# A transformer block on one core: last output chunk by hand, weight norms asked for later, gated values stored as float16 parts, down projection in float16

## The chip, the core and the metric

One core of a Trainium2 chip runs one program. Its engines are TensorE (PE, matrix products), VectorE (DVE), ScalarE (ACT) and GpSimd (POOL); SyncE (SP) issues the transfers that are spoken of here. The metric is the device time of one execution in microseconds (us), as the median of the runs shown.

## The reference, cut to what matters

One layer of a block with two mixing paths and a gated MLP, over 2048 latent tokens of width 1024, with 256 context tokens beside them. The inputs are float32.

```python
h  = modulate(x, norm1_g, sh1, sc1)                 # RMSNorm, scale, shift
...                                                 # attention and delta rule -> o_attn, o_gdn
lat_out = jnp.concatenate([o_attn, o_gdn], axis=-1) @ w_out      # 1024 x 1024
x = x + g1 * lat_out
x = x + g2 * conv_ffn(modulate(x, norm2_g, sh2, sc2), w_up, ffn_conv_w, ffn_conv_b, w_down)
return rms_norm(x, final_norm_g)

def conv_ffn(h, w_up, conv_w, conv_b, w_down):      # w_up 1024 x 5632, w_down 2816 x 1024
    u = depthwise_conv(h @ w_up, conv_w) + conv_b   # width 3 over tokens, centred
    gate, val = jnp.split(u, 2, axis=-1)
    return (jax.nn.silu(gate) * val) @ w_down
```

The change lies in the last three stages: output projection, up projection with conv and gate, down projection with the final norm.

## The kernel before

Everything is kept transposed: 128 features on the partitions, tokens along the free axis. The tokens are cut into four chunks of 512; `cb`, `b` and `k` count blocks of 128 features. A float32 factor is held as two parts, `hi` and `lo` (the rounding error of `hi`), and a product is three matmuls: hi·hi, hi·lo, lo·hi (`prods`; L522, L523, L524 in the down projection).

**Output projection** (`output`, recorded by `Plan`, issued by a planner through L404, which is the line of everything that it issues). For each chunk, in the order 1, 2, 0, 3, and each block `cb`: 24 float32r matmuls into `po`, the gated residual into `xv` (DVE), squares for the second norm. The weights come as `raw_o` and are split into `ws_o` by ACT and POOL. `norm_tail` normalises a finished chunk and writes it to `h2c` in DRAM. During chunk 3, `early` builds seven operand blocks `blk0` for the first 1024 tokens: `B11 T2 T1 B21 T3 T4 B22`, made of sums and differences of `h2c` chunks 0 and 1 and each split into two float16 parts. `late_blocks` builds `blk1` for the other 1024 tokens in the second up step.

**Up projection** (`up_stage`, order written by hand). Step (j, sb) computes gate block j and value block j of 128 hidden features for 1024 tokens; there are 44 steps. Instead of eight 512-column block products it does seven (a Winograd form of Strassen's scheme): P1, P6, P4, P3, P5, P2, P7, of 12 float16 matmuls of 512 columns each (`product`, L1829), where P4 and P3 belong to the step before. Their sums go from the banks `ua`, `ub`, `uc` into the rows `ue` (in the trace part of `xa`). `after` then applies the conv as three taps (ACT L1896, DVE L1899), the gate (ACT L1905, DVE L1906), and stores the float32 product in `hidc` (L1907). `prep` gets the weights of the next j ready beside it, one `next(work)` per product: squares of the two loads `raw_u` on ACT (L1585), their sum over partitions by one PE matmul into `uns` (L1588), a scale by it, and seven sums of quarters, each split by ACT and POOL into `ws_u` (`put`, `split`, L1574 and L1577). `fetch_up` loads the next `raw_u` once `prep` of a j is through. Three buffers are there for `raw`, four for `ws`.

**Down projection**. `units` are (chunk, block b, part): per chunk 8 blocks, each of 22 k in parts of 8, 8 and 6. `fetch` loads a unit's weights `raw_d` two units ahead, `leading` (ACT) and `rest` (DVE) split them into float32r parts `ws_d`. `load_part` loads the gated values of a chunk, one k at a time, as `hraw`, and splits each into `hid` (ACT L1815, DVE or POOL L1816). At the end of a chunk `last_norm` squares, sums (`nps_f`, PE), spreads the reciprocal root over the partitions (`nrs_f`, PE) and scales (`finish`); the program drains it at the end of the next unit group. The final chunk is 514 columns wide (the conv reaches over) and is worked in two cuts.

A generator's `next` writes its next piece into the program. Each engine works through its own instructions in the order in which they were written; SP's transfers are one queue.

## Time and profile before

The kernel takes 3633.89 us (median of 3 runs, 3632.43 to 3639.54). The profiled execution took 3634.78 us, its span is 3633.0.

| what | profiled execution |
|---|---|
| granted clock, mean | 0.947 |
| PE busy | 3252.4 us, 90% |
| weight loads (PEld) | 2300.8 us, 63% |
| DVE busy | 2264.1 us, 62% |
| ACT busy | 1727.6 us, 48% |
| POOL busy | 1656.3 us, 46% |
| moved | 374.96 MB, 103 GB/s |
| input projection, attention, delta rule | 0 to about 1755 us |
| output projection, chunks 1, 2, 0 | to 1970.5 us |
| chunk 3 and up steps one to three | 1970.5 to 2150.4 us |
| rest of the up projection | 2150.4 to 3018.8 us |
| down projection (first matmuls inside the stage before) | 2999.8 to 3633.0 us |

How to read it: a busy share is the time in which an engine had an instruction running, so a PE that runs at a low granted clock is busy as well; the clock is given as a share of the full one. In a listing, `out<-in` are the names of the buffers, `<-ACT junk L1585` after a time in brackets is the idle time just before the instruction and what ended it, and L-numbers are lines of the kernel.

### The profile page before, as it was taken

Reading aid. Unit: us, or ns where it says so; the run is one execution under the profiler, and the core shown is the slowest. Engines: PE = TensorE matmul, PEld = TensorE weight load, DVE = VectorE, ACT = ScalarE, POOL = GpSimd, SP = SyncE. Lnnn points to the kernel's source line nnn. Section 1 sums busy time; section 2 is a strip of 40 time slices with the busy share of each in tenths; the row PEclk is TensorE's granted clock in tenths of the full one; section 3 lists DMA queues with packets and bytes.
Section 4 is the critical chain, followed back from the end, with each engine's and each line's share of the span. In section 5 each row is a group of like instructions: output and inputs, shape, how many; then the busy total and the mean of one; then the engine's idle time right before and its main releaser. Section 6 shows DMA issues by size and latency. Waiting matters only on the chain.

```text
span 3633.0 us, 63480 instructions
## 1 busy us (share of the span) xinstructions
PE 3252.4 (90%) x25544; PEld 2300.8 (63%) x25544; DVE 2264.1 (62%) x3403; ACT 1727.6 (48%) x2676; POOL 1656.3 (46%) x1494
## 2 busy tenths in 40 slices
PE   6899999889999999999788579999989996987988
PEld 3799788757777777776566334444434444766878
DVE  5664678787777788887455655665655654334343
ACT  5442333467777777776434543444334433222231
POOL 5684555557777777777554432233322221000000
PEclk8899999999999999999899789999999998988999
DMA  6222435622222233221355421111111124444452
GB/s 225 86 73 87 134 121 159 185 92 71 75 96 67 98 103 92 85 79 56 125 195 208 147 70 47 47 53 47 53 58 47 47 73 129 125 151 147 128 163 88
DMA packets 217366, 374.96 MB, mean 103 GB/s; under 512 B 21368, under 2 KB 96728, under 8 KB 216800
## 3 DMA queue, kind: packets, MB, share of 16 engines
q1 hardware_dynamic: 215120, 365.50, 31.2%
q0 software_dynamic: 1952, 5.42, 0.6%
q8 instruction: 200, 3.28, 0.4%
q14 instruction: 94, 0.77, 0.1%
HBM read 260.06 MB, written 111.20 MB: 102 GB/s over the span
## 4 chain that ended last, share of the span: by engine, by line
PE 57%; DVE 17%; DMA 11%; POOL 6%; ACT 5%; issue 3%; SPq 1%; POOLq 0%; ACTq 0%; DVEq 0%
PE uc L1829 6%; PE sc L404 6%; PE ub L1829 5%; PE ops L404 5%; DVE cv L1899 4%; PE pdn L522 4%; PE pdn L524 4%; PE pdn L523 4%; PE po L404 4%; DMA hraw<-hidc 3%; DMA raw_u<-in_wu 3%; PE ua L1829 3%; PE sm L404 2%; PE pa L404 1%; DVE mx L404 1%
## 5 line engine op out<-in xcount | busy, mean ns | idle before, releaser
L404 POOL TENSOR_TENSOR lp<-p,hp 128x1024 f16<-128x1024 f32 x288 | 622.0, 2168 | 215.5 <-DVE hp L404 68.7
L1829 PEld LDWEIGHTS <-ws_u 128*128 128x128 f16 x3696 | 374.3, 102 | 504.2 <-issue 82.4
L404 DVE TENSOR_REDUCE mx<-sm 128x1 f32<-128x512 f32 x512 | 336.6, 682 | 65.8 <-PE sm L404 64.0
L404 ACT ACTIVATE p<-sc 128x1024 f32<-128x1024 f32 x288 | 295.3, 1025 | 138.8 <-PE sc L404 124.7
L522 PE MATMUL pdn<-hid,ws_d 128*128 128x512 f32 (+2 forms) x880 | 319.0, 363 | 20.8 <-ACT hid L1815 20.7
L523 PE MATMUL pdn<-hid,ws_d 128*128 128x512 f32 (+2 forms) x880 | 315.0, 358 | 5.6 <-DVE hid L1816 3.3
L524 PE MATMUL pdn<-hid,ws_d 128*128 128x512 f32 (+2 forms) x880 | 313.6, 356 | 0.0
L1899 DVE SCALAR_TENSOR_TENSOR cv<-xa,ufw,cv 128x1024 f32<-128x1024 f32 (+1 forms) x176 | 258.9, 1472 | 66.5 <-ACT cv L1896 63.3
L1829 PE MATMUL ua<-blk,ws_u 128*128 128x512 f16 x1056 | 246.1, 383 | 13.2 <-ACT blk L1574 7.5
L1816 POOL TENSOR_TENSOR hid<-hraw,hid 128x512 fp32r<-128x512 f32 (+1 forms) x24 | 29.3, 1220 | 476.7 <-ACT hid L1815 456.0
L404 PE MATMUL sc<-q,kh 128*128 128x512 f16 x576 | 219.0, 380 | 4.7 <-ACT p L404 3.5
L404 PE MATMUL sc<-qx,kx 128*128 128x512 f16 x576 | 219.2, 381 | 0.0
L404 PE MATMUL po<-ol,ws_o 128*128 128x512 f32 x768 | 201.1, 422 | 15.1 <-ACT ws_o L404 9.0
L1577 POOL TENSOR_TENSOR ws_u<-raw_u,ws_u 128x512 f16<-128x512 f32 x105 | 143.4, 1374 | 149.0 <-ACT ws_u L1574 149.0
L1896 ACT ACTIVATE cv<-xa,cols,ufw 128x1024 f32<-128x1024 f32 (+1 forms) x88 | 108.6, 1238 | 206.6 <-DVE xa L1887 201.8
L522 PEld LDWEIGHTS pdn<-hid,ws_d 128*128 128x128 f32 x880 | 170.6, 194 | 50.9 <-ACT hid L1815 25.8
L404 ACT CAST hp<-p 128x1024 f16<-128x1024 f32 x192 | 201.1, 1048 | 3.6
L404 PE MATMUL ops<-vst,hp 128*128 128x65 f16 (+1 forms) x4608 | 192.5, 194 | 7.0 <-DVE hp L404 3.3
L523 PEld LDWEIGHTS pdn<-hid,ws_d 128*128 128x128 f32 x880 | 170.5, 194 | 36.2 <-DVE hid L1816 7.4
L404 PEld LDWEIGHTS po<-ol,ws_o 128*128 128x128 f32 x768 | 154.3, 204 | 55.9 <-ACT ws_o L404 9.4
L404 PEld LDWEIGHTS <-hp 128*128 128x128 f16 x4608 | 170.6, 98 | 24.1 <-DVE hp L404 5.0
L524 PEld LDWEIGHTS pdn<-hid,ws_d 128*128 128x128 f32 x880 | 170.3, 194 | 23.4
(666 smaller groups left out, 8153.2 us busy)
## 6 DMA issues: line engine op xcount, KB each, us to landing
raw_d<-in_wd SPq DMA_DIRECT2D x64, 512.0 KB
raw_u<-in_wu SPq DMA_DIRECT2D x44, 512.0 KB
tk<-gsc SPq DMA_DIRECT2D x34, 512.0 KB
tT<-gsc SPq DMA_DIRECT2D x66, 256.0 KB
hraw<-hidc SPq DMA_DIRECT2D x66, 256.0 KB
wm<-in_wm SPq DMA_DIRECT2D x64, 256.0 KB
gsc<-kd SPq DMA_DIRECT2D x64, 256.0 KB
raw_o<-in_wo SPq DMA_DIRECT2D x32, 512.0 KB
```

Of the source, the lines that this page charges most:

```text
L404: fn(**{k: v.get() if isinstance(v, Lazy) else v for k, v in kw.items()})
L522: PE.matmul(out=ps, lhsT=hi_l(k), rhs=hi_r(k), start=st, stop=False)
L523: PE.matmul(out=ps, lhsT=hi_l(k), rhs=lo_r(k), start=False, stop=False)
L524: PE.matmul(out=ps, lhsT=lo_l(k), rhs=hi_r(k), start=False, stop=en)
L1577: lo_e.tensor_tensor(out=dst[1], in0=src, in1=dst[0], op=ALU.subtract)
L1816: (G if k % 3 == 2 else V).tensor_tensor(out=at[:, 1, k, :W], in0=raw, in1=at[:, 0, k, :W].bitcast(F32), op=ALU.subtract)
L1829: PE.matmul(out=ps, lhsT=w[:, x, k, :], rhs=b[:, y, k, :], start=first and k + f == 0, stop=k == 3 and f == 2, skip_group_check=True)
L1896: S.activation(out=c, in_=t[:, 0:W], func=AF.Identity, scale=s.fw[:, 3 * r:3 * r + 1], bias=cols[:, C_FB + b:C_FB + b + 1])
L1899: V.scalar_tensor_tensor(out=c, in0=t[:, i:i + W], scalar=s.fw[:, 3 * r + i:3 * r + i + 1], in1=c, op0=ALU.mult, op1=ALU.add)
```

## The change

It has these parts.

- *Output projection.* The planned part does chunks 1, 0, 2. Chunk 3 is written by hand (`last_output`): after every second k of its matmuls come one step of three generators, which build `blk0` in two groups of k (`blocks`), do the norm of chunk 2 and the weights of j = 0, and the scales of j = 1.
- *Up projection.* `prep` becomes `scales` and `parts_of`; two `next` per product are taken, not one. `scales` squares, then idles four calls before `uns`, adds 16 matmuls that give each weight column's norm, idles three calls, and scales. The loads `raw_u` are written earlier, and 22 loads `raw_n` of 512 KB (`wd_squares`) give the norms of the down weights' rows.
- *Gated values.* From the column norms comes a bound `bet` of each gated row; the conv's taps of the value rows are scaled by it, and `after` stores the product as two float16 parts. The second 1024 tokens' rows are one column wider; that column, 511 of chunk 1, is kept in `tailc`.
- *Down projection.* The weights are multiplied by `wds` (DVE, L1935) and split into float16 parts, fetched three units ahead; `raw` has four buffers. `load_hid` fetches a chunk's values, a chunk ahead, in four transfers without a split; for chunk 1 it copies `tailc` into column 511. Only the last block is cut in two. `last_norm` has empty calls between its pieces. The output is stored one column to the right, with single-column stores at the chunk borders.

The diff, cut to this:

```diff
-    RAWB, WSB, OLW = 3, 4, 514
+    RAWB, WSB, XW = 4, 4, 514
...
+    def scales(j, tag):
...
+            junk.append(s3.tile([P, 2, 4, P], BF16, tag=tag, name=f"junk_{j}_{r}", bufs=2))
+            S.activation(out=junk[r], in_=t, func=AF.Square, accum_out=ss[:, r:r + 1])
+            yield
+        yield from idle(4)
+        ps = pt3.tile([P, 512], F32, tag="pt", name=f"uns_{j}")
+        PE.matmul(out=ps[:, 0:2], lhsT=ones, rhs=ss, start=True, stop=True, skip_group_check=True)
+        for r in range(2):
+            for k in range(8):
+                PE.matmul(out=ps[:, 2 + 2 * r:4 + 2 * r], lhsT=junk[r][:, k // 4, k % 4, :], rhs=ones16, ...)
...
+        yield from idle(3)
+        for t in (g, v):
+            S.activation(out=t, in_=t, func=AF.Copy, scale=sg[:, 3:4])
+            yield
...
+    def last_output(xv2, acc2, ol, xv, ready):
...
+        first = chained(blocks(0, blk, 0, True), blocks(0, blk, 1, True))
+        second = chained(idle(4), norm_tail(direct, xv2, 2, acc2, s3, h2c[2], 3), scales(0, "osq"), idle(1), parts_of(0))
+        third = chained(idle(19), scales(1, "osq"))
...
+                if k % 2:
+                    next(first, None)
+                    next(second, None)
+                    next(third, None)
...
     def leading(u):
-            made[u] = w3.tile([P, 2, 8, P], F32R, tag="ws", name=f"ws_d{tb}_{b}_{a}", bufs=WSB)
+            made[u] = w3.tile([P, 2, 8, P], F16, tag="ws", name=f"ws_d{tb}_{b}_{a}", bufs=WSB)
+            V.tensor_tensor(out=raws[u][:, :n], in0=raws[u][:, :n], in1=wds[:, a:a + n].unsqueeze(2).broadcast_to([P, n, P]),
+                            op=ALU.mult)
             S.copy(out=made[u][:, 0, :n], in_=raws[u][:, :n])
...
-            fetch(u + 2)
+            fetch(u + 3)
...
+    def load_hid(c, i):
...
+        if c == 1:
+            for t, a, n in got:
+                V.tensor_copy(out=t[:, 0:n, :, 511], in_=tailc[:, a:a + n, :])
...
     def after(s):
...
-            SY.dma_start(out=hidc[s.j, :, 1024 * s.sb:1024 * s.sb + W], in_=cv[1])
+            z = c.bitcast(F16).rearrange("p (f t) -> p f t", f=2)
+            S.copy(out=z[:, 0, :W], in_=v)
+            V.tensor_tensor(out=z[:, 1, :W], in0=v, in1=z[:, 0, :W], op=ALU.subtract)
+            if sb:
+                G.tensor_copy(out=tailc[:, j, :], in_=z[:, :, 0])
+            for i in range(2):
+                SY.dma_start(out=hidc[2 * sb + i, :, j], in_=z[:, :, sb + 512 * i:sb + 512 * i + 512])
...
+            elif n >= 4 and sb == 0 and j < NJ - 3:
+                drain(work)
+                if n == 4:
+                    fetch_up(3)
+                work = chained(idle(4 if n == 4 else 0), made_up(j + 1), wd_squares(j))
...
     def last_norm(x2, tb, acc):
-        ps = norm_sums(psn, "nps", acc, 512, f"f{tb}")
-        yield
-        rs = rep_rstd(Direct(nc), psn, "nps", 1, s4, 2, ps, 512, f"f{tb}")
-        yield
-        finish(x2, tb, (0, 512), rs)
-        yield
+        yield
+        ps = sums(psn, "nps", acc, 512, f"f{tb}")
+        dg = rstd_made(direct, s4[0], ps, 512, f"f{tb}")
+        yield
+        yield
+        rs = rstd_spread(direct, psn, "nps", 1, dg, 512, f"f{tb}")
+        yield
+        finish(x2, tb, (0, 512), rs, range(0, 4))
+        yield
+        finish(x2, tb, (0, 512), rs, range(4, KT))
+        yield
...
+        load_hid(1, 0)
+        load_hid(1, 1)
         for u, (tb, b, a, n) in enumerate(units):
...
+                if b == 0:
+                    if 0 < tb < NCH - 1:
+                        load_hid(tb + 1, 0)
+                        load_hid(tb + 1, 1)
```

In the order of the instructions this shows at three places. A row is line, operation, `out<-in` with the number of each buffer, and shape; x2 stands for two in a row.

PE in step (3, 0), before: the norm of the weights j = 4 (`uns_4`, of `uss_4`) between the last product into `ub` of step (2, 1) and its last into `uc`.

```order
L1829 LDWEIGHTS ws_u2_1_30230
L1829 MATMUL ub_2_1_30536<-xb_29933,ws_u2_1_30230 128x512
L1588 MATMUL uns_4_30698<-uss_4_30663,k32_76 128x2
L1829 LDWEIGHTS ws_u2_1_30230
L1829 MATMUL uc_2_1_30589<-xa_29796,ws_u2_1_30230 128x512
```

PE there, after:

```order
L1998 LDWEIGHTS ws_u2_1_30363
L1998 MATMUL uc_2_1_30675<-xa_29815,ws_u2_1_30363 128x512
L1753 MATMUL uns_4_30807<-uss_4_30755,k32_76 128x2
L1756 LDWEIGHTS junk_4_0_30758
L1756 MATMUL uns_4_30807<-ones16_27906,junk_4_0_30758 128x2
```

The norm now stands one product later, behind `uc`, and 16 small matmuls with the squares `junk` follow it.

SP about the same steps, before: the stores of gated values (`hidc`) and the weights' loads (`raw_u`).

```order
L1907 DMA hidc_71<-cv_3_1_1_31001 128x1026
L1907 DMA hidc_71<-cv_4_0_1_31132 128x1024
L1630 DMA raw_u6_0_31157<-in_wu 128x1024
L1630 DMA raw_u6_1_31158<-in_wu 128x1024
L1907 DMA hidc_71<-cv_4_1_1_31266 128x1026
```

SP there, after:

```order
L2085 DMA hidc_71<-cv_3_0_0_30975 128x2x512 x2
L2085 DMA hidc_71<-cv_3_1_0_31102 128x2x512 x2
L1738 DMA raw_u6_0_31257<-in_wu 128x1024
L1738 DMA raw_u6_1_31259<-in_wu 128x1024
L2097 DMA raw_n4_31279<-in_wd 128x8x128
L2085 DMA hidc_71<-cv_4_0_0_31274 128x2x512 x2
```

The loads of j = 6 moved ahead of the store of step (4, 0), the load `raw_n4` stands behind them, and each store is two.

DVE at the border of the up and the down projection, before: the last taps (`cv_21`), sums of the last step, and splits of gated values loaded for chunk 0 (`hid_0`).

```order
L1899 SCALAR_TENSOR_TENSOR cv_21_0_1_35645<-xa_29796,ufw_21_35170,cv_21_0_1_35645 128x1024 x2
L1906 TENSOR_TENSOR cv_21_0_1_35645<-cv_21_0_0_35619,cv_21_0_1_35645 128x1024
L1878 TENSOR_TENSOR u3_21_1_35682<-ub_21_1_35557,s1_21_1_35542 128x512
L1879 TENSOR_TENSOR xa_29796<-uc_21_1_35632,u3_21_1_35682 128x512
L1883 TENSOR_TENSOR xa_29796<-ub_21_1_35557,s1_21_1_35542 128x512
L1887 TENSOR_TENSOR xa_29796<-uc_21_1_35632,u2_21_1_35570 128x512
L1816 TENSOR_TENSOR hid_0_1_35711<-hraw_0_8_35712,hid_0_1_35711 128x512
```

DVE there, after:

```order
L2055 TENSOR_TENSOR xa_29815<-uc_21_1_36330,u2_21_1_36298 128x512
L2069 SCALAR_TENSOR_TENSOR cv_21_1_0_36417<-xa_29815,ufw_21_35735,cv_21_1_0_36417 128x1025 x2
L2069 SCALAR_TENSOR_TENSOR cv_21_1_1_36421<-xa_29815,ufw_21_35735,cv_21_1_1_36421 128x1025
L1967 COPY hid_1_36443<-tailc_27907 128x32
L2069 SCALAR_TENSOR_TENSOR cv_21_1_1_36421<-xa_29815,ufw_21_35735,cv_21_1_1_36421 128x1025
L1967 COPY hid_1_B22_36447<-tailc_27907 128x8
L2077 TENSOR_TENSOR cv_21_1_1_36421<-cv_21_1_0_36417,cv_21_1_1_36421 128x1025
L2081 TENSOR_TENSOR cv_21_1_0_36417<-cv_21_1_1_36421,cv_21_1_0_36417 128x1025
L1967 COPY hid_1_hx_36448<-tailc_27907 128x4
L1935 TENSOR_TENSOR raw_d0_0_16_36139<-raw_d0_0_16_36139,wds_27932 128x768
L1942 TENSOR_TENSOR ws_d0_0_16_36458<-raw_d0_0_16_36139,ws_d0_0_16_36458 128x768
```

The splits of gated values are gone; between the last taps stand three copies of `tailc` into the buffers of chunk 1, and behind them the weights of the third unit. PE has at this place the products of the last step, with the first two units of the down projection (43 matmuls into `pdn_0_0`) between P7 and the last two, P4 and P3.

More of the change, by code (lines that the diff above doesn't have):

```diff
@@ L1779, in output @@
-        plan.issue(dict(o=("work", 1.0)))
-        up_w[0] = {m: t.get() for m, t in at.items()}, fw.get()
-        return xv.get(), acc.get(), {m: t.get() for m, t in blk0.items()}
+            if n < 2:
+                pend = norm_tail(plan, xv, tb, acc, s3, h2_l[tb])
+        for _ in range(2):
+            ready.append(weights(*wts.pop(0)))
+        x_end = mk(x3, [P, KT, 512], F32, "x", "x3_3", 2)
+        for k in range(0, KT, 2):
+            SY.dma_start(out=x_end[:, k:k + 2, :], in_=xt[3][:, k:k + 2, :])
@@ new lines, in output, with chained, idle, fetch_up @@
+        plan.keep([xv, acc, nxt, x_end] + ready)
+        plan.issue(dict(o=("work", 1.0)))
+        return xv.get(), acc.get(), nxt.get(), x_end.get(), [w.get() for w in ready]
+    def chained(*gens):
+        for x in gens:
+            yield from x
+    def idle(n):
+        for _ in range(n):
+            yield
+    up_w, raw_u = {}, {}
+    def fetch_up(j, rs=range(2)):
+        if j < NJ:
+            for r in rs:
+                t = w3.tile([P, 2, 4, P], F32, tag="raw", name=f"raw_u{j}_{r}", bufs=RAWB)
+                raw_u.setdefault(j, []).append(t)
+                SY.dma_start(out=t.rearrange("p a k f -> p (a k) f"), in_=wu[2 * j + r])
@@ new lines, in staged, with put, plain @@
+    def staged(sb, n, tb, k0):
+        t = s3.tile([P, 3, 512], F32, tag="oraw", name=f"hst{sb}_{n}_{k0}", bufs=3)[:, 0:2, :]
+        SY.dma_start(out=t, in_=h2c[tb, :, k0:k0 + 2, :])
+        return t
+    def put(blk, n, kp, x, eng):
+        split(eng, [blk[n][:, f, 2 * kp:2 * kp + 2] for f in range(2)], x)
+    def plain(sb, blk, which):
+        got = []
+        for n, kp in which:
+            tb, k0 = dict(B11=(0, 0), B21=(0, 4), B22=(1, 4))[n]
+            got.append((n, kp, staged(sb, "p" + n, 2 * sb + tb, k0 + 2 * kp)))
+            if len(got) == 2:
+                yield
+                put(blk, *got.pop(0), V)
+        yield
+        put(blk, *got.pop(0), V)
+        yield
@@ L1824, in up_stage @@
     def up_stage():
+        xv2, acc2, ol, xv, ready = output(Plan(tc, psn, pt3, ps3), x3, s3)
+        acc, blk0, rest0, work = last_output(xv2, acc2, ol, xv, ready)
         def product(ps, w, b, first):
@@ L1937, in late_blocks, with drain, made_up @@
+        def drain(g):
+            for _ in g:
+                pass
+        def made_up(j):
+            yield from scales(j, "nacc")
+            yield from parts_of(j)
+            fetch_up(j + 1)
             yield
-        first = norm_tail(direct, xv_, NCH - 1, acc_, s3, h2c[NCH - 1])
-        carry = w3.tile([P, 2 * NJ, 2], F32, name="carry", bufs=1)
-        xa = x3.tile([P, KT, OLW], F32, tag="x", name="xa").rearrange("p a t -> p (a t)")
+        tail = norm_tail(direct, xv, 3, acc, s3, h2c[3], 2)
```

636 lines of the change are left out of this document (352 added, 284 removed).

## The prediction

> **What bounds the kernel now.** I read the busy time by stage first: last output chunk with the first up-projection steps, the steady up projection, their border with the down projection, the down projection.
>
> ```profile
> 1970.50:2140.00 169.50, 109.56 (x398) 62.99 (x399) 102.14 (x119) 78.92 (x114) 78.17 (x54) 0.80 0.42 141
> 2140.00:2999.80 859.80, 799.73 (x3532) 355.46 (x3533) 505.74 (x555) 347.58 (x467) 253.75 (x345) 0.95 0.16 53
> 3018.80:3633.00 614.20, 525.36 (x2661) 440.19 (x2659) 226.39 (x294) 156.31 (x214) 34.05 (x27) 0.92 0.44 133
> ```
>
> After the stretch come its length, then busy time of PE, weight loads, DVE, ACT and POOL, the clock, and the DMA share. PE is the busiest everywhere, and a granted clock below 1 says that it also ran slowly. So I ask what each stage would take at PE's pace, then what stops PE. The pace comes from the timeline of PE, whose columns are start and duration.
>
> ```profile
> 2150.42 1.89 PE L1829 MATMUL ua<-blk,ws_u 128*128 128x512 f16 x8
> ...
> 2179.70 0.59 PE L1588 MATMUL uns<-uss,k 128*128 128x2 f32 x2 [3.21 <-ACT junk L1585]
> 2180.14 5.28 PE L1829 MATMUL uc<-xa,ws_u 128*128 128x512 f16 x12
> ...
> 2463.76 2.75 PE L1829 MATMUL ub<-blk,ws_u 128*128 128x512 f16 x12
> 2466.35 2.75 PE L1829 MATMUL ub<-xb,ws_u 128*128 128x512 f16 x12
> 2472.29 0.38 PE L1588 MATMUL uns<-uss,k 128*128 128x2 f32 x2 [3.19 <-ACT junk L1585]
> 2472.53 4.44 PE L1829 MATMUL uc<-xa,ws_u 128*128 128x512 f16 x12
> ...
> 3066.16 0.40 PE L522 MATMUL pdn<-hid,ws_d 128*128 128x512 f32 x1
> ...
> 3072.17 0.39 PE L524 MATMUL pdn<-hid,ws_d 128*128 128x512 f32 x1
> ...
> 3616.56 0.28 PE L522 MATMUL pdn<-hid,ws_d 128*128 128x256 f32 x1
> ...
> 3618.21 0.28 PE L524 MATMUL pdn<-hid,ws_d 128*128 128x256 f32 x1
> ```
>
> A float16 matmul of 512 columns takes 2.59/12 = 0.2158 us; a float32r one 6.01/26 = 0.2312; a float32r one of 256 columns 1.65/14 = 0.118. The norm `uns` makes PE wait 3.2 us, and the product behind it takes 4.44 to 5.28 us, not 2.59.
>
> What PE waited for, by stage (transition, up, down; total, times, longest):
>
> ```profile
> PE po L404 <- ACT ws_o L404: 9.0, 1, 9.0
> ...
> PE uns L1588 <- ACT junk L1585: 63.1, 20, 3.5
> ...
> PE nrs_f L488 <- DVE ndg_f L486: 29.4, 3, 11.1
> PE nps_f L506 <- DVE nacc_f L498: 22.3, 3, 8.3
> PE pdn L522 <- ACT hid L1815: 20.7, 8, 11.4
> ```
>
> In steady up steps `uns` is the only wait; in down it is three final norms and the splitting of loaded gated values.
>
> **The parts, one by one.** The sum runs along PE, against the profiled execution's own span of 3633.0.
>
> *Weight norms asked for later.* The last of the 21 `uns` lies at 2933.3 (two instructions, the second is below): from j=3 to j=21, 18 periods of (2933.3 − 2179.7)/18 = 41.87 us, against 168 × 0.2158 = 36.25 of products. So 5.6 us per j go to this norm.
>
> ```profile
> L1588 PE MATMUL uns<-uss,k x42: 251/352/374, 2066.7 to 2933.6; 128*128 128x2 f32 x42
> ```
>
> How it comes, by the queue and ACT in the same j:
>
> ```profile
> 2445.31 19.39 SPq L1907 DMA_DIRECT2D hidc<-cv  x2
> 2464.80 1.20 SPq L1630 DMA_DIRECT2D raw_u<-in_wu  x2
> ...
> 2469.82 1.06 ACT L1585 ACTIVATE junk<-raw_u 128x1024 bf16<-128x1024 f32 x1 [5.28 <-DMA raw_u<-in_wu]
> ...
> 2471.09 1.06 ACT L1585 ACTIVATE junk<-raw_u 128x1024 bf16<-128x1024 f32 x1
> ```
>
> The fetch stands on SP behind a store that waits for DVE, so the first load lands 5.0 us after 2464.80, more than three products into the step that squares it, and PE asks for the norm behind the third (2466.35 + 2.59). After, the fetch is written into the third product of the step before; its second load waits for POOL's last split, by my count some 12 us into that step of 18.9, and lands at 17. PE asks behind the fourth product. The squares begin when ACT has copied the first product (2.6 + 0.6 us into the step) and take 2 × 1.27: done at 5.8, asked for at 10.4. The wait goes, with 4.6 us to spare. If that cover is gone, it is because SP stands at a load whose buffer POOL still reads: behind `raw_u` and `raw_n` the store `hidc` queues, and for the store the next `cv` buffer on ACT. Added on PE: 16 small matmuls.
>
> ```profile
> 1603.23 0.40 PE L404 MATMUL ops<-vst,lp 128*128 128x65 f16 x8
> 1603.46 0.66 PE L404 MATMUL ops<-vst,hp 128*128 128x65 f16 x16
> ```
>
> The nearest rows give 0.23 us for eight, 0.46 for 16; with the old one, whose next product starts 0.24 us behind it, 0.7 per j. From step four (2150.42 now) to the stage's end 41 × 84 + 24 = 3468 products remain: 748.4 + 19 × 0.7 = 761.7. Now it is 3018.8 − 2150.4 less 8.4 us of down matmuls that lie inside, 860.0:
>
> ```profile
> 2999.83 0.59 PE L522 MATMUL pdn<-hid,ws_d 128*128 128x512 f32 x1
> ...
> 3007.81 0.39 PE L524 MATMUL pdn<-hid,ws_d 128*128 128x512 f32 x1
> ```
>
> Saved 98.
>
> *More work on DVE and ACT in each step.* The stored float16 parts add one subtraction of 128x1024 and one cast per step, the scales nine tiny operations per j.
>
> ```profile
> L1577 DVE TENSOR_TENSOR blk<-hst_b,blk 128x1024 f16<-128x1024 f32 x4 | 4.9, 1225 | 6.2 <-ACT blk L1574 6.2
> ...
> L404 DVE TENSOR_TENSOR us<-us,raw_u 128x512 f32<-128x512 f32 x1 | 1.6, 1628 | 1.0 <-POOL ws_u L404 1.0
> ...
> L1613 DVE TENSOR_TENSOR us<-us,raw_u 128x512 f32<-128x512 f32 x1 | 0.7, 684 | 0.0
> ```
>
> DVE now is busy 505.74/859.8 = 59%, 24.6 us per j; 2 × 1.23 + about 1.6 more make 28.7 of 37.0 us, 78%. I cost it at nothing: PE needs the old sum of bank `ub` only two products into the next step, 5.2 us after DVE may start it. The 22 loads `raw_n` (512 KB each) and their squares lie beside a DMA share of 0.16.
>
> *Last output chunk by hand, blocks of chunks 0 and 1 beside it.* Now it takes 2150.4 − 1970.5 = 179.9 us to the end of the third step.
>
> ```profile
> 1970.50 0.53 PE L404 MATMUL po<-ol,ws_o 128*128 128x512 f32 x1
> ```
>
> PE's own work there: 192 × 0.2312 + 228 × 0.2158 = 93.6, with the small matmuls about 100. After, DVE has to do in the chunk 16 subtractions and splits of 1.23 us, eight gated sums and eight norm products of 0.74, seven sums of 0.6, four weight operations of 0.68 and the scales' small ones, 44 us; 17 in the first step, 28 in the second, up to the block T2 that the third step's second product needs. That is 89 us, and it begins some 10 us in (2 MB of `raw_o` and 1.5 MB of `h2c` come first, at the 347 GB/s that the fullest stretch shows, below). PE alone would get there in 44.4 + 13 + 18.1 + 2.6 and some 6 of small matmuls, 84. So at least 15 us of stall. The two rows of `us` show the same operation at 684 and, with POOL at work beside it, at 1628 ns; and today's stretch stalls 80. I take 40, ends 15 and 80: 140 us. Saved 40.
>
> ```profile
> 1860.00:1880.00 20.00, 16.06 (x66) 12.42 (x65) 11.23 (x14) 9.47 (x16) 9.82 (x8) 0.91 0.97 347
> ```
>
> The Trainium skill (SBUF — State Buffer, the section on two separate sides) calls the port pair of DVE and GpSimd an exclusive lock, held for a whole instruction; the two rows agree. By that rule alone, DVE's two-input operations and POOL's splits of the chunk would stand one behind the other, near 60 us, and the stall would be about 30: within my ends.
>
> *Down projection in float16.* Now 1584 × 0.2312 + 1056 × 0.118 = 490.8; after 2046 × 0.2158 + 132 × 0.118 = 457.1. Saved 33.7. The Trainium skill (TensorE: Matmul & The Clock Gate, the section on 56 ns) gives 215.7 ns for any warm 512-column matmul: by it float32r would be as quick as float16 and this term zero. The rows show 231.2, so the measurement decides.
>
> *Gated values loaded ready, final norms spread over four calls.* Now the stage lasts 614.2 + 8.4 = 622.6: 490.8 of matmuls, 14.5 of tail (from 3618.5 in the next rows to 3633.0; unchanged), 117.3 of waits, norm matmuls and slow clock. After, a chunk's 5.8 MB come in four transfers a chunk ahead, and the norms ask for sums one unit (5 us) late: I leave 6 us for the norms' matmuls, an estimate of less than one product (2.59 us) each. A new multiplication per unit (1.23 us, DVE) lies beside 5.2 us of matmuls.
>
> ```profile
> L1896 ACT ACTIVATE cv<-xa,cols,ufw 128x1024 f32<-128x1024 f32 (+1 forms) x88 | 108.6, 1238 | 206.6 <-DVE xa L1887 201.8 <-POOL carry L1902 4.5
> L1906 DVE TENSOR_TENSOR cv<-cv,cv 128x1024 f32<-128x1024 f32 (+1 forms) x44 | 69.7, 1585 | 4.5
> L1574 ACT CAST blk<-hst_b 128x1024 f16<-128x1024 f32 x8 | 8.4, 1044 | 19.4 <-DVE hst_b L1929 10.2 <-DMA hst_b<-h2c 8.6 <-DVE hst_b L1924 0.6
> L2037 DVE SCALAR_TENSOR_TENSOR x<-x,cols,nrs_f 128x512 f32<-128x512 f32 x24 | 16.1, 742 | 3.3 <-PE nrs_f L488 3.3
> ...
> 2482.12 2.60 DVE L1899 SCALAR_TENSOR_TENSOR cv<-xa,ufw,cv 128x1026 f32<-128x1026 f32 x2
> ...
> 3618.53 0.48 DVE L2083 SCALAR_TENSOR_TENSOR x<-pdn,mod,x1p 128x256 f32<-128x256 f32 x1 [0.45 <-PE pdn L524]
> ```
>
> One wait is new, and DVE's rows in the section on the change show it: at the stage's start copies of `tailc` into `hid_1` stand ahead of the weights of the third unit. The first two wait for 4.2 and 1 MB that start only when PE leaves block B21; the third for a load behind the last store. After PE's last product comes DVE's sum 0.7, ACT's first tap 1.24, DVE's four taps 5.2 and product 1.6, ACT's cast 1.04, DVE's subtraction 1.23, store and load (estimated at 3, below the 5.0 us of a 512 KB load), multiplication and cast of six blocks 1.8: 15.8 us in all, and PE has 1 us of work left. With some ten matmuls at about half pace, as behind `uns`, that is 17 us; ends 10 (copies free) and 30 (the loads at 70% of 347 GB/s). Down becomes 457.1 + 14.5 + 6 + 17 = 494.6; saved 128.
>
> *Edits at nothing.* Chunk order 1, 0, 2: same work in the planned part. The output shifted by one column: six stores of single columns, nobody waits for them. The float16 `wds` and `scale_wd` chain: one small matmul. At the chunk borders 5.8 MB stand ahead of `raw_d`; 16.6 us at 347 GB/s against three units in advance: I leave 8 for all, ends 0 and 24.
>
> **Sum.** 3633.0 − 98 − 40 − 128 + 8 = 3375 for the span; the time is 1.8 above the span in this execution (3634.78), and the median of the runs (3633.89) lies 0.9 below that: 3376.
>
> **Rivals.**
> - *DVE sets the pace of the up steps.* For it: 78% busy in order, and 1628 instead of 684 ns where POOL runs. Against: steady rows stay short, and only `uns` stalls PE today. At 20.5 us per step rather than 18.5: 41 × 2 = 82, 3458.
> - *The norm wait stays*, `raw_u` late behind `raw_n` on SP. Then 19 × 5.6 = 106: 3482. Against: the later load is issued some 10 us before its use.
> - *The down stage becomes bound by transfers.* A chunk moves 5.8 + 11.5 + 2.1 + 2.1 = 21.5 MB; at 161 GB/s, what the stage reached at a share of 0.53, that is 133 us against 116: 4 × 17 = 68, 3444. Against: 347 GB/s above.
>
> ```profile
> 3300.00:3400.00 100.00, 80.85 (x325) 64.11 (x324) 41.05 (x53) 30.02 (x42) 8.91 (x7) 0.88 0.53 161
> ```
>
> - *float16 brings no pace*: 3376 + 34 = 3410. Against: both rates stand above.
> - *Slower: POOL's port doubles DVE's operations through both stages.* DVE's operations with two inputs from SBUF, 20 us per j (taps 11.8, products 3.2, subtractions 2.5, weights 2.7), would double: 49 us per j against 37, 20.5 × 12 = 246; in down 9.1 us per 14.3 become 16.7, 32 × 2.4 = 77. 3699. It decides once steady `us` rows go beyond 1.5 us; today they show 0.69.
> - *Better*: transition and border at their low ends, 3376 − 25 − 7 − 8 = 3336.
>
> **Numbers.** Forecast (3340 to 3410) 0.65; DVE pace 0.10; transfers 0.08; norm wait 0.06; no float16 pace 0.02; better than 3340 0.06; slower 0.03. The range takes the bounds: 3336 below; above, the transition at no gain and the border at 30 give 3429, and I go on to 3455 for the two cheaper rivals. What cannot be told from no change is 0.2%, 7 us; faster 0.95, the same 0.01, slower 0.04.
>
> **What will show it.** No `uns` wait among PE's waits, and 37 us from one `uns` to the next; float16 `pdn` 0.216 apart; one gap of 15 to 20 us about 1 us behind the last `uc`, ended by ACT or DVE `ws_d`; no waits of `nps_f`/`nrs_f`; 140 us from the first `po` of chunk 3 to the end of step three. I am wrong if PE waits for DVE in steady steps, or if chunk borders show gaps that end on `raw_d`.

## The result, and the profile after

The changed kernel takes 3465.17 us (median of 4 runs, 3461.13 to 3465.49), 0.9529 of the kernel before (95% interval 0.9513 to 0.9546). The profiled execution took 3465.49 us, its span is 3463.7. So 169 us were saved where 258 were forecast, and the time lies 10 us above the range's upper end of 3455.

The stretches of the changed kernel, last output chunk with three up steps, rest of the up projection, down projection, columns as before; below them the first of these in the kernel before:

```profile
1971.60:2147.80 176.20, 119.92 (x494) 69.14 (x495) 110.54 (x142) 83.70 (x109) 67.17 (x50) 0.80 0.43 146
2147.80:2975.60 827.80, 781.27 (x3856) 357.07 (x3855) 557.22 (x778) 405.85 (x544) 274.73 (x387) 0.99 0.23 79
2975.60:3463.70 488.10, 457.07 (x2178) 214.44 (x2176) 278.43 (x321) 115.64 (x131) 7.10 (x6) 0.97 0.47 153
```

```profile
1970.50:2150.40 179.90, 119.96 (x446) 67.73 (x447) 108.37 (x127) 85.41 (x121) 79.64 (x61) 0.81 0.39 133
```

9.3 us of down matmuls (the row of 43 below) lie inside the second stretch. Against the sum of the forecast:

| term | forecast | measured | miss |
|---|---|---|---|
| first product of chunk 3 | 1970.5 | 1971.6 | 1.1 |
| to the end of step three | 140 | 176.2 | 36.2 |
| rest of the up projection | 761.7 | 827.8 − 9.3 = 818.5 | 56.8 |
| down projection with border | 494.6 | 488.1 + 9.3 = 497.4 | 2.8 |
| allowance for small edits | 8 | none seen | −8 |

Together 88.9, the distance from 3375 to 3463.7 but for rounding. Two terms failed, by 93.0 us together; the allowance, which nothing needed, hides 8 of them. The down projection did not fail. Its rows on PE's timeline, 48 float16 matmuls in 10.36 us (0.2158 each), and the border:

```profile
3304.11 10.52 PE L2264 MATMUL pdn<-hid,ws_d 128*128 128x512 f16 x48
3314.47 4.05 PE L2264 MATMUL pdn<-hid_T,ws_d 128*128 128x512 f16 x18
```

```profile
2961.15 9.44 PE L2264 MATMUL pdn<-hid,ws_d 128*128 128x512 f16 x43
...
2975.61 1.24 PE L2264 MATMUL pdn<-hid,ws_d 128*128 128x512 f16 x5
2995.36 2.88 PE L2264 MATMUL pdn<-hid_T,ws_d 128*128 128x512 f16 x6 [18.51 <-ACT ws_d L1937]
```

What PE waited for in the second stretch (all rows; total us, times, longest):

```profile
PE ub L1998 <- DVE xa L2046: 34.6, 20, 6.6
PE wdn L1980 <- DVE wdo L1976: 7.7, 1, 7.7
PE uns L1753 <- ACT junk L1749: 2.6, 2, 2.3
PE ub L1998 <- POOL ws_u L1609: 1.5, 2, 0.8
```

The 63.1 us for `uns` are down to 2.6, and a new wait has come, for DVE's sum that frees bank `ub`. These four rows are 46 of the 57 us. Behind five of the waits, those of 2.3 us and more, the next product took 4.20 to 4.37 us instead of 2.59, which makes 8.4 more.

Why the sum is late, in one steady step of PE and DVE:

```profile
2397.64 2.75 PE L1998 MATMUL ub<-xb,ws_u 128*128 128x512 f16 x12
2400.23 2.75 PE L1998 MATMUL ua<-blk,ws_u 128*128 128x512 f16 x12
2402.82 2.75 PE L1998 MATMUL ub<-blk,ws_u 128*128 128x512 f16 x12
2406.81 2.75 PE L1998 MATMUL ub<-xb,ws_u 128*128 128x512 f16 x12 [1.24 <-DVE xa L2046]
```

```profile
2395.52 1.63 DVE L1804 TENSOR_TENSOR raw_u<-raw_u,ws_u 128x512 f32<-128x512 f32 x1 [1.83 <-POOL ws_u L1609]
...
2399.71 5.12 DVE L2069 SCALAR_TENSOR_TENSOR cv<-xa,ufw,cv 128x1024 f32<-128x1024 f32 x4 [1.36 <-ACT cv L2066]
2404.93 1.23 DVE L2077 TENSOR_TENSOR cv<-cv,cv 128x1024 f32<-128x1024 f32 x1
2406.08 0.68 DVE L2046 TENSOR_TENSOR xa<-ub,s 128x512 f32<-128x512 f32 x1
```

P7 (the first row) had left bank `ub` at 2400.2, and PE wants it back two products later, at 2405.4. DVE could read it from 2400.2 on, but the taps of the step before and the gate's product stand ahead in its queue, and the taps had begun only at 2399.7, behind a weight difference (L1804) that waited for POOL. Taps and product take 6.4 us, so the sum ends at 2406.76. The 5.2 us of cover are used up by DVE's own queue, and PE waits 1.24 us.

### The profile page after: what moved, and what is told of

Its sections match the earlier page's. It is cut to its first block, busy times and chain, and to the rows that moved or that the text cites. A ratio compares the mean times of both kernels' runs of the same rounds, so it can differ in the third digit from the quotient of the medians.

```text
span 3463.7 us, 63363 instructions
## 1 busy us (share of the span) xinstructions
PE 3164.4 (91%) x25434; PEld 2075.3 (60%) x25434; DVE 2365.3 (68%) x3668; ACT 1741.3 (50%) x2655; POOL 1636.3 (47%) x1504
## 4 chain that ended last, share of the span: by engine, by line
PE 49%; DVE 20%; issue 10%; POOL 9%; ACT 6%; DMA 6%; SPq 0%; POOLq 0%; DVEq 0%; ACTq 0%
PE pdn L2264 13%; PE sc L404 6%; DVE cv L2069 6%; PE ops L404 5%; PE po L404 4%; PE sm L404 3%; POOL ws_u L1609 2%; PE ub L1998 2%; ACT cv L2066 1%; PE pa L404 1%; DVE mx L404 1%; DMA wm<-in_wm 1%; ACT junk L1749 1%; DVE oraw L404 1%; DMA hst_b<-h2c 1%
## 5 line engine op out<-in xcount | busy, mean ns | idle before, releaser
L1998 PEld LDWEIGHTS <-ws_u 128*128 128x128 f16 x3696 | 364.0, 99 | 511.3 <-issue 84.7
L2264 PEld LDWEIGHTS <-ws_d 128*128 128x128 f16 x2178 | 213.3, 98 | 264.5 <-ACT ws_d L1937 19.0
L2264 PE MATMUL pdn<-hid,ws_d 128*128 128x512 f16 (+1 forms) x1584 | 337.8, 373 | 0.0
L2069 DVE SCALAR_TENSOR_TENSOR cv<-xa,ufw,cv 128x1024 f32<-128x1024 f32 (+1 forms) x172 | 223.6, 1311 | 71.9 <-ACT cv L2066 65.8
L1937 ACT CAST ws_d<-raw_d 128x1024 f16<-128x1024 f32 (+1 forms) x96 | 93.5, 974 | 268.1 <-DVE raw_d L1935 223.6
L404 PE MATMUL sm<-kh,q 128*128 128x512 f16 x512 | 174.4, 383 | 10.0 <-DVE mx L404 9.2
L1942 DVE TENSOR_TENSOR ws_d<-raw_d,ws_d 128x1024 f16<-128x1024 f32 (+1 forms) x96 | 108.8, 1134 | 79.2 <-ACT ws_d L1937 79.2
L404 PE MATMUL po<-ol,ws_o 128*128 128x512 f32 x576 | 151.9, 423 | 7.5 <-POOL ws_o L404 6.4
L522 PE MATMUL pg<-hl,ws_g 128*128 128x512 f32 x384 | 152.9, 398 | 0.0
L524 PE MATMUL pg<-hl,ws_g 128*128 128x512 f32 x384 | 152.5, 397 | 0.0
L523 PE MATMUL pg<-hl,ws_g 128*128 128x512 f32 x384 | 151.8, 395 | 0.0
```

The source lines that it names most:

```text
L404: fn(**{k: v.get() if isinstance(v, Lazy) else v for k, v in kw.items()})
L522: PE.matmul(out=ps, lhsT=hi_l(k), rhs=hi_r(k), start=st, stop=False)
L523: PE.matmul(out=ps, lhsT=hi_l(k), rhs=lo_r(k), start=False, stop=False)
L524: PE.matmul(out=ps, lhsT=lo_l(k), rhs=hi_r(k), start=False, stop=en)
L1937: S.copy(out=made[u][:, 0, :n], in_=raws[u][:, :n])
L1942: V.tensor_tensor(out=made[u][:, 1, :n], in0=raws[u][:, :n], in1=made[u][:, 0, :n], op=ALU.subtract)
```

## Experiments

Each run is the changed kernel with the edit shown, unless said otherwise. "Stretch" is the time from the first product of chunk 3 to the end of step three (176.2 us in the changed kernel). Each stretch is read from one trace. Six traces of kernels that are alike in this stretch, the changed kernel's among them, give 175.2 to 176.4, so about a microsecond either way says nothing.

**Ask for the norm early again.** The loads stay early.

```diff
-        yield from idle(4)
+        yield from idle(4 if j < 4 or j > NJ - 3 else 0)
...
-        yield from idle(3)
+        yield from idle(3 if j < 4 or j > NJ - 3 else 7)
```

> In the changed kernel the four idle calls ahead of the norm `uns` are taken out for j = 4 to 19 (four are put behind it, so that the rest stays where it was); the early loads of `raw_u` stay. Theory (the place in PE's order makes the norm free, and early loads alone would not): PE then asks for `uns` behind the second product of the step, where ACT is still at its squares, which end about 4.4 us later; `uns` waits 3 to 4.5 us again, the product behind it runs at the lower clock, and the period per j goes from 38.2 to 42 to 44 us: 3525 to 3560 us in all. Rival (the early loads took the wait away, the place does not matter): no `uns` wait over 1 us, 3465 us within 5.

3520.91 us, ratio 0.9685 (0.9672 to 0.9698): 55.7 us lost. PE's timeline in this run, from one steady norm to the next:

```profile
2428.91 0.51 PE L1753 MATMUL uns<-uss,k 128*128 128x2 f32 x2 [2.66 <-ACT junk L1749]
2429.28 0.56 PE L1756 MATMUL uns<-ones,junk 128*128 128x2 bf16 x16
2429.71 4.08 PE L1998 MATMUL ub<-xb,ws_u 128*128 128x512 f16 x12
2433.63 0.59 PE L1998 MATMUL uc<-xa,ws_u 128*128 128x512 f16 x2
...
2470.12 0.59 PE L1753 MATMUL uns<-uss,k 128*128 128x2 f32 x2 [2.66 <-ACT junk L1749]
```

The wait is back: 2.66 or 2.67 us at 14 of the 15 steady norms, and 2.94 at one. The product behind it takes 3.92 us from start to start here and 3.92 to 5.07 at the others. A j takes 41.2 us between the two rows and 41.7 on average, a little under the 42 expected, since the wait for `ub` is gone from these steps. So early loads alone do not make the norm free; they do so together with its place in PE's order. Whether the place would be enough with late loads, no run shows.

**Copy to `tailc` on DVE, not POOL.**

```diff
-                G.tensor_copy(out=tailc[:, j, :], in_=z[:, :, 0])
+                V.tensor_copy(out=tailc[:, j, :], in_=z[:, :, 0])
```

> In the changed kernel the copy of column 511 into `tailc` goes from POOL to DVE. In steady steps PE waits 1.24 us per j for DVE's sum of `ub` (L2046). Theory P (POOL starts it: it stands at the copy until DVE's subtraction is done, 3 us with weight splits queued behind it, so DVE waits for those splits, then the taps and the sum are late): the splits start about 3 us earlier, the wait of 1.24 us per j goes, period 38.2 to 37.0 us, 3440 to 3448 us in all. Theory D (DVE's own load and order delay the sum): the wait stays between 0.8 and 1.5 us, 3460 to 3470 us.

3464.61 us, ratio 0.9535 (0.9521 to 0.9549): no change by the times. The steady wait for L2046 falls only from 1.24 to 1.07 us, and the total in the second stretch from 34.6 to 31.9. POOL's stand at that copy is real, but it is not what makes the sum late.

**Sums ahead of the gate's product.**

```diff
             S.activation(out=f, in_=f, func=AF.Silu)
+            if 2 < j < NJ - 2:
+                yield
```

> In the changed kernel one more call is put ahead of the gate's product (L2077) for j = 3 to 19, so that DVE does the sums of `ub` and `uc` of the next step ahead of that product; the same work in another order. Theory D (the sum is late because the product of 1.23 us stands ahead of it in DVE's queue): the wait of 1.24 us per j goes or falls below 0.3, 3443 to 3450 us, and the 6.6 us wait at the end of the stage falls by about 1. Rival (DVE has too much work per step, and order does not help): the wait turns up at another product of the step, 3460 to 3470 us.

3442.32 us, ratio 0.9468 (0.9455 to 0.9481): 22.9 us gained with the same work. Of PE's waits for that sum 12.3 us are left, five waits near both ends, and on PE's timeline two steady norms lie 36.80 us apart:

```profile
PE ub L1998 <- DVE xa L2046: 12.3, 5, 6.1
```

```profile
2404.84 0.54 PE L1756 MATMUL uns<-ones,junk 128*128 128x2 bf16 x16
...
2441.64 0.54 PE L1756 MATMUL uns<-ones,junk 128*128 128x2 bf16 x16
```

So DVE is not short of time in a steady step; the order of its queue was at fault. 36.80 − 36.26 = 0.54 us is the whole price of a norm with its 16 matmuls (0.7 forecast).

**Down weights ahead of the last taps.**

```diff
+        leading(2)
+        rest(2)
         P4(prev)
         P3(prev)
+        for u in (3, 4):
+            leading(u)
+            rest(u)
...
+            if u == 8:
+                for t, a8, n8 in ends:
+                    V.tensor_copy(out=t[:, 0:n8, :, 511], in_=tailc[:, a8:a8 + n8, :])
```

> In the changed kernel the weights of units three, four and five of the down projection are written ahead of the last step's taps, and the copies of `tailc` into the buffers of chunk 1 are put eight units later; the same work. Theory (the stall of 18.5 us at the border is DVE's queue: last taps, copies that wait for loads, then weights): PE's longest wait there falls below 5 us, 3445 to 3451 us in all. Rival (the transfers of chunk 1 at this place set it, since 5.8 MB are loaded at once and the weights' loads stand behind them): the stall moves to a later unit as a wait for `raw_d` and less than half of it is saved, 3456 to 3466 us.

3456.22 us, ratio 0.952 (0.9501 to 0.9538): 9 us less by the median and by the trace, but the interval overlaps that of the changed kernel (its five runs lie between 3454.64 and 3469.24), so the times alone do not show a gain. The trace shows what moved: of the 18.5 us of stall 10.75 are left, and they stand later; PE, DVE and SP's queue there:

```profile
3000.21 6.07 PE L2273 MATMUL pdn<-hid_T,ws_d 128*128 128x512 f16 x16 [10.75 <-DVE ws_d L1942]
```

```profile
2998.54 0.75 DVE L2278 SCALAR_TENSOR_TENSOR x<-pdn,mod,x1p 128x512 f32<-128x512 f32 x1 [7.51 <-DMA x1p<-x1c]
```

```profile
2991.06 0.89 SPq L2084 DMA_DIRECT2D hidc<-cv  x2
2994.11 0.33 SPq L1964 DMA_DIRECT2D hid_hx<-hidc  x1
2994.49 0.90 SPq L2254 DMA_DIRECT2D x1p<-x1c  x2
```

Neither theory had this: the residual of the first block, `x1p`, stands on SP behind the last store, and DVE stands at it with the weights of unit six behind. That points to the order of the transfers and not to their size; the combined run below, which puts these loads ahead of the last stores, has no such stall.

**First loads of `h2c` ahead of `raw_o`.**

```diff
+        first = chained(blocks(0, blk, 0, True), blocks(0, blk, 1, True))
+        next(first)
         for cb in range(3, 7):
             load(cb)
-        first = chained(blocks(0, blk, 0, True), blocks(0, blk, 1, True))
```

> In the changed kernel's last output chunk the first three loads of `h2c` (`hst_b`) are issued ahead of the four loads `raw_o`, not behind them; DVE waits 10.75 us for them there, PE 9.7 us for the spread of chunk 2's norm (`nrs_b`), and the second load of the group stands on SP behind `raw_u`, which waits 15.5 us for a buffer. Theory Q (the order on SP's queue sets the transition): the wait of `nrs_b` falls to 4 us or less, the next wait (`uns`, 13.6 us) to under 8, and the end of the third up step comes 10 to 18 us sooner: 3447 to 3455 us in all. Rival C (the end is set by the chain behind chunk 3's last output product: its norm, store, load, blocks): the early waits shrink but that end moves by less than 5 us, 3460 to 3466 us.

3463.77 us, ratio 0.952 (0.9505 to 0.9535), stretch 175.5. DVE's first split begins 5.6 us into the stretch, not 12.2, but the wait for `nrs_b` is still 8.9 us and that for `uns` grows to 16.3: the start is given back at the second group's loads, where ACT waits 7.6 us for the load and DVE 11.3 for ACT's cast. The end does not move, as the rival had it.

**Norm of the down weights later.**

```diff
-                work = chained(*(wd_squares(q) for q in range(NJ - 3, NJ)), idle(1), scale_wd())
+                work = chained(*(wd_squares(q) for q in range(NJ - 3, NJ)))
...
             elif (j, sb) == (NJ - 2, 1):
                 drain(work)
+                work = scale_wd()
```

> In the changed kernel the norm of the down weights (`wdn`, one matmul, and the scales behind it) is asked for one step later, in step (20, 1); PE waits 7.7 us for it now. Theory: nobody needs its result before step (21, 1), so the wait and the slow product behind it go: 3454 to 3459 us in all. Rival (the wait comes back at the border, since the weights of units one and two then wait for `wds`): 3463 to 3467 us.

3457.12 us, ratio 0.9492 (0.9475 to 0.9508): 8 us gained. The wait falls from 7.7 to 2.9 us; nothing comes back at the border (18.7 us for `ws_d`, 18.5 before). In the combined run below the same order leaves a wait of 6.0 us, so the place is not yet far enough behind.

**Final norms without empty calls** (three `yield` lines out of `last_norm`).

> In the changed kernel the three empty calls of `last_norm` are taken out, so that sums and spread of a chunk's final norm are asked for at once, as before the change. Theory (the empty calls hide the norms, as the forecast had it): the waits for `nps_f` and `nrs_f` come back, 29.4 + 22.3 us before the change, and with the slow clock behind them 45 to 65 us are lost: 3510 to 3530 us. Rival (the norms' waits went because DVE has less to do in the down projection, not by the calls): under 15 us are lost, up to 3480 us.

3485.79 us, ratio 0.9572 (0.9558 to 0.9586): 20.6 us lost, between the two theories. Of PE's waits in the down projection, the one that is new, and the timeline at one of its three places:

```profile
PE nrs_f L1582 <- DVE ndg_f L1577: 9.0, 3, 3.0
```

```profile
3112.20 2.05 PE L1582 MATMUL nrs_f<-ndg_f,k 128*128 128x512 f32 x2 [2.97 <-DVE ndg_f L1577]
3114.04 7.21 PE L2261 MATMUL pdn<-hid,ws_d 128*128 128x512 f16 x24
3121.09 1.24 PE L2261 MATMUL pdn<-hid_B,ws_d 128*128 128x512 f16 x5
```

3.0 us a chunk for the spread, and behind it 24 matmuls in 7.05 us instead of 5.18; the sums `nps_f` (22.3 us before) cost nothing even so. The empty calls are worth 21 us. The rest of the norms' old waits stayed away without them; that it went with the split of gated values from DVE's queue fits, but no run shows it alone.

**Norm of chunk 3 faster** (two more `next(extra, None)` per product in the first up step).

> In the changed kernel's first up step the norm of chunk 3 is written with four calls per product instead of two, so that its eight pieces stand ahead of the weights of j = 1 and of the other blocks on DVE and ACT; the same work. Theory C (the end of the third step is set by the chain behind chunk 3: norm, store, load, blocks, up to the 13.7 us wait for block T2): `h2c` is stored 5 to 8 us sooner, and that wait falls by as much: 3457 to 3461 us. Rival (DVE and ACT are the limit as such, what comes first makes the other late): the wait for weights (`ws_u`, 3.3 us) grows by what the other loses, 3462 to 3468 us.

3464.19 us, ratio 0.9512 (0.9498 to 0.9527), stretch 171.7. By the trace 4.5 us sooner, by the times not told from no change; PE's wait for T2 stays (14.2 us), and the second wait for `nrs_b` grows from 1.2 to 4.8.

**Taps of the first step left out.**

```diff
-                for i in (1, 2):
+                for i in () if (j, sb) == (0, 0) else (1, 2):
```

> In the changed kernel the four tap operations of DVE in the first up step (j = 0, first 1024 tokens; 8.8 us, the conv of this block is left out but for one tap) are not done. They stand on DVE between the two groups of `blk1`, in the 30 us between the landing of the first loads of `h2c` chunk 3 and the 13.7 us wait of PE for block T2. Theory W (in this stretch DVE's work sets the pace, 28 of 31 us busy): T2 is ready 7 to 9 us sooner and PE's wait falls to 5 to 7 us: 3455 to 3460 us in all. Rival L (the loads of the second group and the casts of ACT set it): the wait falls by less than 3 us, 3461 to 3466 us.

3461.66 us, ratio 0.9516 (0.9503 to 0.9529), stretch 172.7; T2's wait 11.4 us. DVE with 8.8 us less to do now waits itself, for ACT and then for the loads of the second group:

```profile
2119.16 1.23 DVE L2077 TENSOR_TENSOR xa<-xa 128x1024 f32<-128x1024 f32 x1 [4.72 <-ACT xa L2076]
2121.15 1.23 DVE L1840 TENSOR_TENSOR hst_b<-hst_b,hst_b 128x1024 f32<-128x1024 f32 x1 [0.76 <-DMA hst_b<-h2c]
2123.41 1.23 DVE L1842 TENSOR_TENSOR hst_b<-hst_b,hst_b 128x1024 f32<-128x1024 f32 x1 [1.03 <-DMA hst_b<-h2c]
```

DVE's work alone does not set it.

**Queue order**: first loads ahead as above, and `fetch_up` at `k == 6`, not at `k == 2`.

> As the run with the first loads of `h2c` ahead, and the four loads `raw_u` of the last output chunk are written behind the loads of `h2c` of the same block `cb` (at k = 6, not k = 2), so that no load of `h2c` stands on SP behind one that waits for a buffer of POOL's splits. Theory Q (the early stalls of the transition come from SP's queue): the waits of `uns` (13.6 to 16.3 us) and `nrs_b` (8.9) fall together by 8 us or more, and the end of the third step comes 5 to 10 us sooner: 3453 to 3460 us. Rival C (the chain of DVE and ACT work behind it gives the time back): under 4 us, 3461 to 3466 us.

3463.01 us, ratio 0.952 (0.9507 to 0.9533), stretch 171.9: 4.3 us by the trace, where 5 to 10 were expected; the waits for `uns` and `nrs_b` together fell by 1.3 us only.

**Combined**: sums first, down weights' norm later, border, `x1p` of the first two blocks ahead of the last stores, queue order.

> The changed kernel with the sums ahead of the gate's product, the down weights' norm one step later, the weights of units three to five ahead of the last taps, the loads of the first two residual blocks (`x1p`) put ahead of the last stores (in an unused part of a buffer of chunk 0), and the queue order of the run before. Theory (the gains lie at different places and add): 23 for the sums, 8 for the norm, 14 to 16 for the border (the stall of 10.7 us that stayed in the border run falls to about 4), 0 to 8 for the queue: 3410 to 3422 us. Rival (one gives back what another gains, as DVE is the common limit): 3430 to 3445 us.

3414.35 us, ratio 0.9383 (0.937 to 0.9396): 50.8 us below the changed kernel, so the gains add. The border's stall is gone, 1.7 us are left in three waits. The stretch is 173.5 us, where the queue order alone gave 171.9 with the same instructions in it.

**Norm of chunk 2 behind the weights of j = 0**, on top of the combined kernel. (Its stretch, put at 176.1 in the expectation, is 173.5 by its rows.)

```diff
-        second = chained(idle(4), norm_tail(direct, xv2, 2, acc2, s3, h2c[2], 3), scales(0, "osq"), idle(1), parts_of(0))
-        third = chained(idle(19), scales(1, "osq"))
+        second = chained(idle(12), scales(0, "osq"), idle(1), parts_of(0))
+        third = chained(idle(20), scales(1, "osq"))
+        fourth = chained(idle(17), norm_tail(direct, xv2, 2, acc2, s3, h2c[2], 3))
```

> The combined kernel with the norm of chunk 2 put behind the weights of j = 0 in the last output chunk (its steps begin at call 18, not 5; the scales of j = 0 at call 13, not 18), the same work. In the combined run PE waits 8.4 us for the spread `nrs_b` of this norm and 12.8 us for `uns`, whose squares stand on ACT behind the eight pieces of that norm. Theory C (these two waits come from the norm's place in the order, and what they cost is paid at the end of the chain behind chunk 3): `nrs_b` falls to under 3 us, `uns` to under 8, and the stretch from chunk 3's first product to the end of the third up step, 176.1 us in the combined run, falls by 6 to 14: 3400 to 3409 us in all. Rival (DVE's and ACT's work and waits for loads in the stretch as such set its end): the stretch falls by less than 3 us, and other waits, of `nps_b`, `ws_u` or T2, grow: 3411 to 3417 us.

3409.71 us, ratio 0.9372 (0.9357 to 0.9387), stretch 167.9, 5.6 us less. The wait for `uns` falls from 12.8 to 6.0; that for `nrs_b` (9.8) does not, `nps_b` grows from 3.8 to 7.4 us, a wait for DVE's sum of `ub` in the second step from 2.3 to 7.7, and T2's is 13.7 (14.6). Half of each theory; by the times (the intervals overlap) it is not told from the combined kernel.

**Five staging buffers**, on top of that: for the second 1024 tokens the second group's `b11` and `b22` are loaded into two `raw` buffers, T3 is built ahead of T1, both T4 last.

> The kernel of the run before (norm of chunk 2 later), with the blocks of the second 1024 tokens built from five staging buffers instead of three (two of the weights' `raw` buffers, idle there), so that the loads of the second group need not wait until the first is used up, with T3 ahead of T1 and the two T4 last. Theory S (the staging buffers hold block T2): PE's wait for T2, 13.7 us, falls by 5 to 9 us, 3400 to 3405 us in all. Rival (DVE's and ACT's sequence holds it): it falls by less than 2 us, 3408 to 3412 us.

3413.71 us, ratio 0.9394 (0.9381 to 0.9407): no gain, and 2.3 us more in the stretch, 170.2. DVE begins the second group at 2110.71, the end of the stretch is 2147.64, and T2's wait on PE's timeline is 7.09 + 3.91 us:

```profile
2124.28 0.59 PE L2040 MATMUL ub<-blk,ws_u 128*128 128x512 f16 x1 [7.09 <-ACT blk L1608]
2128.78 1.44 PE L2040 MATMUL ub<-blk,ws_u 128*128 128x512 f16 x3 [3.91 <-DVE blk L1609]
```

DVE begins the second group 133.3 us into the stretch, not 141.4, so the loads are no longer late. But PE gets the last part of T2 151.3 us in, against 151.4: taps and casts of the first step come between, and the waits of `uns` take the rest (14.2 us, 11.0 before). The buffers were one limit, and DVE's and ACT's sequence stands close behind it.

**Two calls per product in (19, 0), four in (19, 1)**, on top of the kernel with the norm later.

> The kernel with the norm of chunk 2 later, with the weight preparation in step (19, 0) written at two calls per product as in the steps before, and at four in step (19, 1), instead of three in both. Theory (at three calls the weights' sums and splits stand ahead of the sum of `ub` on DVE, PE's 6.1 us wait): that wait falls below 2 us and 4 to 7 us are saved, 3402 to 3406 us. Rival (the preparation that is packed into step (19, 1) makes a wait there, of `uns` or `ub`): 3407 to 3414 us.

3406.19 us, ratio 0.9371 (0.9358 to 0.9383): not told from 0.9372. The 6.1 us wait for `ub` in step (19, 1) goes and one of 5.8 us for `uns` stands in its place, as the rival had it.

The version to keep is the one with the norm of chunk 2 later: ratio 0.9372 (0.9357 to 0.9387) to the kernel before, 55.5 us below the changed kernel. The combined kernel and this last one are as good by the times.

## Why the prediction went wrong, step by step

*Weight norms asked for later*: right in mechanism. PE waits 2.6 us for `uns` in the second stretch instead of 63.1, the early request brings 55.7 us back, and a norm costs 0.54 us (0.7 forecast). The cover was thinner than the 4.6 us counted: in the step above ACT's squares end at 2409.81 and PE asks at 2411.99, 2.2 us later. In the first stretch `uns` waits 17.4 us, where it waited 11.5 before.

*More work on DVE and ACT in each step*: the step that failed most, 57 us. What came is the prediction's own sign of being wrong: PE waits for DVE in steady steps. "I cost it at nothing: PE needs the old sum of bank `ub` only two products into the next step, 5.2 us after DVE may start it." The cover was counted as if DVE were free when the bank is left. Its queue holds 5.12 us of taps and 1.23 of product at that place, so the cover was short by about a microsecond. The rival on DVE's pace named the engine (82 us at 20.5 us per step), but not the cause: 19.1 us per step, and the order, not the amount, since the same work in another order took 23 us off. Near both ends, where weights of two j and the down weights' norm are written close together, the same cover gave way by 2 to 7 us at a time: 14.5 us of the 34.6, and 7.7 for `wdn`, which the text had not priced as a wait at all. One of these was only moved by another pace (6.1 us for `ub` became 5.8 for `uns`); how to lose them is not shown.

*Last output chunk by hand*: 3.7 us saved where 40 were forecast. The stretch took 76 us more than PE's own 100, inside the stated 15 to 80 but nearly twice the 40 taken. PE was busy for 119.92 us of it, against 119.96 before, at a granted clock of 0.80, and stood for 56.3, against 59.9: the waits have other names more than other sizes. The five longest of PE's waits in this stretch of the changed kernel:

```profile
PE uns L1753 <- ACT junk L1749: 17.4, 3, 13.6
PE ub L1998 <- ACT blk L1608: 13.7, 1, 13.7
PE nrs_b L1582 <- DVE ndg_b L1577: 10.9, 2, 9.7
PE nps_b L1589 <- DVE nacc_b L498: 5.0, 1, 5.0
PE ub L1998 <- ACT ws_u L1608: 3.3, 1, 3.3
```

The failed step is the sum that sets DVE's 89 us of work, begun 10 us in and then done without a break, against PE's 84. By it block T2 is ready 99 us into the stretch. PE went on with T2 only 157.9 us in:

```profile
2129.53 0.59 PE L1998 MATMUL ub<-blk,ws_u 128*128 128x512 f16 x1 [13.72 <-ACT blk L1608]
```

```profile
1971.60:2129.50 157.90, 102.73 (x428) 62.02 (x429) 99.05 (x130) 73.86 (x97) 61.21 (x43) 0.80 0.42 146
```

Up to there DVE was busy for 99.05 us, 10 more than counted, and stood for 58.9, where the sum has 10. Its two longest waits up to there:

```profile
DVE blk L1609 <- ACT blk L1608: 30.6, 12, 10.8
DVE hst_b L1840 <- DMA hst_b<-h2c: 9.1, 1, 9.1
```

So about 49 us are waits of DVE for SP, ACT, POOL and PE, which the sum left out. The 99 us are not all work either. Measured against the shortest operation of the same form, about 18 of them are DVE operations that took longer, and each of those has an operation of POOL beside it. Two taps took 4.36 us beside a split on POOL, where four take 5.12 in the steady step above:

```profile
2109.97 4.36 DVE L2069 SCALAR_TENSOR_TENSOR xa<-xa,ufw 128x1024 f32<-128x1024 f32 x2 [1.39 <-ACT xa L2066]
```

```profile
2110.95 2.29 POOL L1609 TENSOR_TENSOR xb<-hst_b,xb 128x1024 f16<-128x1024 f32 x1 [2.12 <-ACT xb L1608]
```

The prediction saw such a pair of rows (684 and 1628 ns) and gave it no price of its own inside the 40. Nor does it set the end alone: without 8.8 us of taps T2's wait fell by 2.3. Six runs each took one of DVE's waits or operations away or moved it, and the stretch changed by −5.6 to +2.3 us. That fits several limits a few us apart; which single order would be best for this stretch stays open.

*Down projection in float16, gated values loaded ready, norms spread*: right. 0.2158 us a matmul, where float32r took 0.2312; no wait for `nps_f` or `nrs_f`; no gap on `raw_d`. The tail stayed at 14.5 us, and the norms took about 5 where 6 were left, so this term is not right by luck. One of its reasons was sized loosely: the empty calls are worth 21 of the 52 us. The Trainium skill (TensorE: Matmul & The Clock Gate, the section on 56 ns) gives 215.7 ns for a warm 512-column matmul and names no type; the float16 rows agree with it, the float32r rows do not.

*The new wait at the border*: 18.5 us in one piece where 15.8 and some slow matmuls were forecast, with the third `tailc` copy waiting 6.60 us for its load. That its cause is order is shown by the two runs together: with the weights moved it shrank to 10.75 us, and with the loads of `x1p` moved as well to 1.7. That SP's queue is part of it was missed.

*POOL's port*, the rival of 3699 us: against it stand the steady rows, in which DVE's 128x512 operation takes 0.68 us, and 1.63 only beside POOL's splits (L1804, about 0.9 us more per j). An operation that reads a bank (L2051, at 2397.08) takes 0.68 us beside the same splits. With the sums put first L1804 still takes 1.63 us, and PE no longer waits in the steady steps. In the last output chunk and the first steps, though, DVE's operations beside POOL's took the 18 us above longer. The exclusive lock of the Trainium skill (SBUF — State Buffer, the section on two separate sides) agrees with these rows; no run here takes POOL's work away.

*The range.* The two misses, 57 and 36, were each in the text, as a rival of 82 and as a bound of 40. The upper end of 3455 is 3429, which has the transition at no gain and the border at 30, and 26 for the rivals; with the 57 us in full it would have been 3486.

## What to carry to other kernels

Cover is counted from when the engine reaches the instruction in its queue, not from when the data are ready: list what stands ahead of it there, with durations, and the longer ones where POOL works beside it. Where engines hand short pieces to each other in order, a sum of one engine's work says little of the end; expect the waits to change names, and price the stretch at no gain unless the trace shows one wait that ends alone. Ask for a reduction several products after its input, and move work that nobody needs soon (last taps, a norm of later weights) behind what the critical engine asks for next: the norm asked for later gave 56 us here, the sums put first 23, the later norm 8; the last taps put behind gave 9 by the medians, which is not clear of the scatter of that run.
